# A new order for the seven products of a Winograd tile in the first feed-forward layer, with the scheduler free to order the pair's instructions

## The chip, the core and the metric

The kernel runs on one core of one Trainium2 chip. A core has four engines that compute, and each works through its own list of instructions in order: TensorE (PE in the rows; PEld are its weight loads), VectorE (DVE), ScalarE (ACT) and GpSimd (POOL). SyncE (SP) only starts transfers; GpSimd starts some too. Matrix products go into PSUM, which the kernel uses as eight tiles of one bank each (128 partitions x 512 fp32). Time is the device time of one launch in microseconds (us). The kernel before took 2807.16 us, the median of 3 runs (2806.87 to 2811.38).

## The reference, cut to what matters

One layer of a diffusion backbone works on 256 latent tokens and 256 context tokens of width 2048. The change lies in the first feed-forward half-step, which both groups of tokens go through with the same weights:

```
gate, up = jnp.split(h @ w_in, 2, axis=-1)        # w_in: 2048 x 11264
return (jax.nn.silu(gate) * up) @ w_out
h  = h  + 0.5 * mod[:, 2] * swiglu(modulate(h,  norm_ffn1, mod[:, 0], mod[:, 1]), w_ffn1_in, w_ffn1_out)
hc = hc + 0.5 * mc[2]     * swiglu(modulate(hc, norm_ffn1, mc[0],  mc[1]),  w_ffn1_in, w_ffn1_out)
```

After it come a mixer (linear attention beside a convolution), a second feed-forward half-step for the latent tokens, and a norm.

## The kernel before, in words

**Products in three passes.** Every fp32 operand is split into a high part that TensorE takes at its fast rate and a low remainder. One product of a 128x128 weight block is three matmuls (`mm3`): high by high, high by low, low by high. For weights, ScalarE casts 128x1024 values into a tile `whi` and VectorE subtracts to get `wlo`; `split_next` does this. There are three such buffers (NW = 3), so the cast for a product can begin when the product three places earlier is through on TensorE.

**The pairs.** Hidden tiles 11 to 43 (33 of the 44 tiles of 128 hidden columns) are computed by `pair_tile`. The two token groups and the two halves of the width make a 2x2 block matrix; gate and up weights by the two halves of the width make another. Winograd's scheme multiplies them with seven products of blocks in place of eight. Each product is 8 weight blocks by 3 matmuls, 24 matmuls of 256 columns. Here the products are called product 0 to product 6 by their place in the order. `plan` (line 864) names for each its bank (`a`, `b` or `c`) and its token factor; `Pair.PARTS` (line 103) names its weight factor. Some token factors are sums, kept in the tiles `s` (only product 4, factor `s3`, reads tiles of that name in this stage).

**Intermediate results.** Bank `a` accumulates across four products and is read in between: `late(i)`, run after product i, copies it to SBUF (`S.copy`) or combines it on VectorE. The next matmuls into `a` must wait until that reading is done.

**Weight factors.** A pair has two raw tiles of 128x2048, unit 0 (gate) and unit 1 (up). `t1` is a ScalarE copy of a gate block to which GpSimd's queue adds an up block by an accumulating transfer; `t2` is `t1` plus the up block "22" by VectorE, and later plus the gate block "21"; `t3` is an accumulating transfer into unit 1. `make_t1` and `make_t3` start these for the next pair while the present one runs. There are four raw slots (NRAW = 4). When a unit is used up, `leave` frees its slot and `load` lets SP fetch the next unit. Between the products of a pair lies a "j" step: one 128x2048 row block of the modulation weights takes a raw slot too, and one VectorE instruction multiplies and sums it (`wide_step`, the tile `wcol`).

**What sets the order.** The program is written step by step: the matmuls of product i, then the cast and subtraction for product i+3, then `late(i)`. A scheduler may move instructions against this order. In the kernel before, `pin[0]` (lines 316 and 321) is set during a pair's steps, and then every instruction that goes through `Clocked` (line 64, which is why nearly all rows carry L64) is kept in program order.

Of the kernel before, what the change touches and what calls it, by code (L numbers as in the profile page):

```python
# [18 lines left out]
KT = 16  # L19
T = 256  # L20
# [79 lines left out]
class Pair:  # L100


    PARTS = ("11", "21", "t1", "t2", "t3", "22", "t4")

    def __init__(self, wg, wu):
        self.units = (Unit(wg, 2048), Unit(wu, 2048))
# [3 lines left out]
        self.up_low = wu[:, 0:1024]  # L110
        self.parts = self.PARTS
        self.t = {}
# [3 lines left out]
def layer_kernel(ctx: ExitStack, tc: tile.TileContext, A):  # L116
    nc = tc.nc
    keep = tc.keep_in_program_order
    pin = [False]
    V, PE, S = (  # L120
        Clocked(e, p, keep, pin)
        for e, p in ((nc.vector, _price_dve), (nc.tensor, _price_pe), (nc.scalar, lambda *a: 0.0))
    )
# [13 lines left out]
    def gt(p="g", dt=F32, shape=(128, 512), n=512):  # L137
        t = gpool.tile([128, 2 * (T + 2)], dt, tag="g", name=nm(p))[:, :n]
        return t if len(shape) == 2 else t.rearrange("p (a t) -> p a t", a=shape[1])

    def pst():
        return pspool.tile([128, 512], F32, tag="ps", name=nm("ps"))
# [19 lines left out]
    def m_load():  # L162
        m = mload
        while m["n"] < min(m["used"] + m["ahead"], len(m["srcs"])):
            raw = mraw()
            nc.sync.dma_start(out=raw, in_=m["srcs"][m["n"]])
            m["raw"][m["n"]] = raw
            m["n"] += 1
# [4 lines left out]
    def run():  # L173
        halves = [(u, i) for k, u, i, _ in steps if k == "w"]
        order, pos = [], 0

        def leave(u):
            nonlocal used
            ring["free"].append(ring["at"].pop(u))
            used += 1  # L180
            return raws.pop(u)
# [23 lines left out]
        def load(upto):  # L205
            nonlocal nload
            while nload < min(upto + ring["n"], len(order)):
                u = order[nload]
                raw = raw_tile(u)
                nc.sync.dma_start(out=raw[:, : u.n], in_=u.src)  # L210
                raws[u] = raw
                nload += 1
# [4 lines left out]
        def block(u, b):  # L217
            raw = raws[u.units[int(b[1]) - 1]]
            o = 1024 * (int(b[0]) - 1)
            return raw[:, o : o + 1024]  # L220
# [26 lines left out]
        def pair_after(u, b):  # L247
            nonlocal used
            if b == "t2":
                V.tensor_tensor(out=u.t["t2"], in0=u.t["t2"], in1=block(u, "21"), op=ALU.add)  # L250
            if b in ("t2", "22"):
                leave(u.units[b == "22"])
                load(used)
                later = order[order.index(u.units[1]) + 1 :][:3]
                for x in later:
                    if x.pair is not None and x.pair is not u:
                        (make_t1 if b == "t2" else make_t3)(x.pair)
                        break

        def split_next(early=False):  # L260
            nonlocal pos, used
            if pos >= len(halves):
                return
            u, i = halves[pos]
            pos += 1
            if isinstance(u, Pair):
                m, src = 1024, factor(u, u.parts[i])
            else:
                h0, m = u.parts[i]
                src = raws[u][:, h0 : h0 + m]  # L270
            b = (pos - 1) % NW
            hi = wpool.tile([128, 1024], F32R, tag=f"whi{b}", bufs=1, name=nm("whi"))
            lo = wpool.tile([128, 1024], F32R, tag=f"wlo{b}", bufs=1, name=nm("wlo"))
            c = S.copy(out=hi[:, :m], in_=src)
            d = V.tensor_tensor(out=lo[:, :m], in0=src, in1=hi[:, :m].bitcast(F32), op=ALU.subtract)
            if early:
                keep(c)
                keep(d)
            ready[u, i] = (hi, lo)
            if isinstance(u, Pair):  # L280
                pair_after(u, u.parts[i])
            elif i == len(u.parts) - 1:
                leave(u)
                for x in order[order.index(u) + 1 :][:3]:
                    if x.pair is not None and x in raws:
                        (make_t1 if x is x.pair.units[0] else make_t3)(x.pair)
                load(used)
# [8 lines left out]
        for k, u, i, fn in steps:  # L296
            late = None
            if k == "p":
                fn()
            elif k == "s":  # L300
                split_next(True)
                begun += 1
            elif k == "j":
                fn(raws[u])
                leave(u)
                load(used)
            elif k == "m":
                fn(mload["raw"].pop(i))
                mload["used"] += 1
                m_load()  # L310
            else:
                while begun < NW:
                    split_next(True)
                    begun += 1
                hi, lo = ready.pop((u, i))
                pin[0] = isinstance(u, Pair)
                late = fn(hi, lo)
                split_next()
                if late:
                    late()  # L320
                pin[0] = False
            if k == "w" and slow:
                rate["credit"] += rate["r"]
                while slow and rate["credit"] >= 1:
                    rate["credit"] -= 1
                    slow.popleft()()
            V.t = max(V.t, PE.t - LAG)
            while bg and V.t + bg[0][0] <= PE.t:
                bg.popleft()[1]()
# [40 lines left out]
    def split(src, n=512):  # L370
        hi, lo = gt("hi", F32R), gt("lo", F32R)
        lows(hi[:, :n], lo[:, :n], src)
        return hi, lo
# [244 lines left out]
    wide = deque((c, k) for c in (6, 7, 5, 8) for k in range(KT))  # L618
# [203 lines left out]
    ps2, s3, qf = {}, {}, {}  # L822
# [38 lines left out]

    def pair_tile(f, wg, wu):
        box = {}
        plan = (("a", "11"), ("c", "12"), ("b", "p"), ("a", "s2"), ("a", "s3"), ("b", "q"), ("a", "22"))

        def late(i):
            a, b, c = (box.get(x) for x in "abc")
            if i == 0:
                box["s"], box["u"] = gt("ps"), gt("pu")
                S.copy(out=box["s"][:, :T], in_=a)  # L870
            elif i == 1:
                t = box["s"][:, :T]
                V.tensor_tensor(out=t, in0=c, in1=t, op=ALU.add)
                S.activation(t, t, AF.Silu)
            elif i == 2:
                S.copy(out=box["u"][:, :T], in_=b)
            elif i == 3:
                S.copy(out=box["s"][:, T:], in_=a)
            elif i == 4:
                t = box["u"][:, :T]  # L880
                V.tensor_tensor(out=t, in0=t, in1=a, op=ALU.subtract)
            elif i == 5:
                t = box["s"]
                p = box["p"] = gt("p")
                V.tensor_tensor(out=t[:, T:], in0=b, in1=t[:, T:], op=ALU.subtract)
                V.tensor_tensor(out=p[:, :T], in0=t[:, :T], in1=t[:, T:], op=ALU.mult)
            else:
                t, p = box["u"], box["p"]
                S.activation(t[:, T:], a, AF.Silu)
                V.tensor_tensor(out=p[:, T:], in0=t[:, :T], in1=t[:, T:], op=ALU.mult)  # L890
                hid[f] = split(p)
                keep_hid(f)
                if f // CH_FT < NCH - 1:
                    del hid[f]

        def part(i):
            key, x = plan[i]

            def fn(hi, lo):
                first = key not in box  # L900
                if first:
                    box[key] = pst()[:, :T]
                for j in range(HK):
                    mm3(box[key], (hi, lo), j * 128, x_factor(x, j), first and j == 0, j == HK - 1, not first)
                return lambda: late(i)

            return fn

        u = Pair(wg, wu)
        for i in range(7):  # L910
            steps.append(("w", u, i, part(i)))
            if i == 3 and len(wide) > 2 * KT:
                wide_step()


# [30 lines left out]
    def keep_hid(f):  # L946
        hi, lo = hid[f]
        hid_d[f] = [dpool.tile([128, 512], F32, tag=f"hid{f}_{i}", name=nm("hidd")) for i in range(2)]
        for d, t in zip(hid_d[f], (hi, lo)):
            nc.gpsimd.dma_start(out=d, in_=t.bitcast(F32))  # L950
# [170 lines left out]
    plan = [(0, c) for c in seq0] + [(1, c) for c in seq1]  # L1121
# [730 lines left out]
    for f in range(2, FT):  # L1852
        a = f < NF2
# [10 lines left out]
    for dt in range(KT):  # L1864
        box = {}
# [38 lines left out]

    P(finish)
    run()


# [121 lines left out]
```

## Time and profile before

| | |
|---|---|
| median of 3 runs | 2807.16 us |
| the profiled execution | 2808.95 us |
| its span, first to last instruction | 2807.1 us |
| TensorE busy in the span | 2699.7 us (96%) |
| VectorE, ScalarE, GpSimd busy | 1878.1, 1119.7, 187.2 us |
| mean granted TensorE clock | 0.98 of full speed |

The profiled execution is one run, 1.8 us above the median; its span leaves 1.85 us outside. The granted clock is 1.00 at 2.4 GHz and 0.50 at 1.2 GHz; a value between them is a stretch that holds both. Ends of matmuls are modelled, so the distance between their starts is the better measure.

### The profile page before, as it was taken

The page shows a single profiled execution, that of the slowest core. Times are in us where ns is not written, and L with a number is a line of the kernel's source. Part 1 is how long each engine was busy: PE and PEld are TensorE (multiplying, and loading weights), DVE is VectorE, ACT ScalarE, POOL GpSimd, SP SyncE. Part 2 cuts the span into 40 slices and gives each one's busy share as a digit, 9 for nine tenths or more (in the row PEclk, how much of TensorE's full clock was granted, in tenths as well). Part 3 has the DMA queues.
Part 4 walks back from the last instruction along what each step waited for, and adds up shares of the span by engine and source line. Part 5 has one row for each costly group of instructions (what it writes and reads, how often), then busy time and mean ns, then how long its engine had stood idle before and what let it go on. Part 6 is the DMA issues. An engine that isn't in the chain of part 4 may idle for free.

```text
span 2807.1 us, 45740 instructions
## 1 busy us (share of the span) xinstructions
PE 2699.7 (96%) x18964; PEld 2488.9 (89%) x18964; DVE 1878.1 (67%) x2553; ACT 1119.7 (40%) x1498; POOL 187.2 (7%) x212
## 2 busy tenths in 40 slices
PE   7999999999999999999999899999999999999998
PEld 5668899999999998888888898879999999999998
DVE  6657866666666665479789897767776655444444
ACT  5234444444444443112112554435554444444443
POOL 0002211111111110001001110000100000000000
PEclk9999999999999999999999999999999999999999
DMA  9844577777677678966986442635557765555553
GB/s 366 300 156 168 141 210 200 210 209 217 202 205 208 203 207 319 393 225 243 396 293 222 164 175 69 216 134 213 183 180 275 282 252 188 188 181 182 189 183 122
DMA packets 126635, 608.33 MB, mean 217 GB/s; under 512 B 14682, under 2 KB 15066, under 8 KB 78172
## 3 DMA queue, kind: packets, MB, share of 16 engines
q1 hardware_dynamic: 109308, 546.69, 55.2%
q0 software_dynamic: 16544, 57.68, 9.4%
q8 instruction: 148, 2.42, 0.3%
q10 hardware_dynamic: 576, 1.05, 0.1%
q14 instruction: 59, 0.48, 0.0%
HBM read 580.20 MB, written 25.17 MB: 216 GB/s over the span
## 4 chain that ended last, share of the span: by engine, by line
PE 32%; issue 27%; DVE 2%; DMA 1%; ACT 0%; POOL 0%; POOLq 0%; DVEq 0%; ACTq 0%
PE ps L64 32%; DVE wlo L64 1%; DMA raw<-in_wg 0%; DVE y L64 0%; DVE junk L64 0%; ACT whi L64 0%; DMA raw<-in_wmodT 0%; DVE E L64 0%; DVE S L64 0%; DVE raw L64 0%; DVE xs L64 0%; POOL h L1901 0%; DVE lo L64 0%; DVE h L64 0%; ACT y L64 0%
## 5 line engine op out<-in xcount | busy, mean ns | idle before, releaser
L64 PE MATMUL ps<-hi,whi 128*128 128x256 f32 (+1 forms) x4736 | 1445.4, 307 | 7.8 <-DVE h L64 3.3
L64 PE MATMUL ps<-lo,whi 128*128 128x256 f32 (+1 forms) x4736 | 1448.5, 306 | 2.7 <-DVE lo L64 2.7
L64 PE MATMUL ps<-hi,wlo 128*128 128x256 f32 (+1 forms) x4736 | 1445.9, 306 | 3.8 <-DVE wlo L64 3.7
L64 DVE TENSOR_TENSOR wlo<-raw,whi 128x1024 fp32r<-128x1024 f32 (+1 forms) x654 | 803.9, 1230 | 662.3 <-ACT whi L64 657.0
L64 ACT CAST whi<-raw 128x1024 fp32r<-128x1024 f32 (+1 forms) x654 | 679.2, 1039 | 1276.7 <-PE ps L64 1239.0
L64 PEld LDWEIGHTS ps<-hi,whi 128*128 128x128 f32 x4736 | 895.1, 189 | 65.7 <-issue 11.9
L64 PEld LDWEIGHTS ps<-lo,whi 128*128 128x128 f32 x4736 | 895.3, 189 | 50.4 <-DVE lo L64 2.9
L64 PEld LDWEIGHTS ps<-hi,wlo 128*128 128x128 f32 x4736 | 893.8, 189 | 49.8 <-DVE wlo L64 4.7
L64 DVE CUSTOM_DVE_ANT_0 junk<-mraw,mraw 128x1024 bf16<-128x1024 f32 x192 | 239.0, 1245 | 6.5 <-DMA mraw<-in_wmodT 2.9
L64 PE MATMUL ps<-hh,wlo 128*128 128x256 f32 x704 | 198.2, 282 | 0.0
L64 PE MATMUL ps<-hh,whi 128*128 128x256 f32 x704 | 197.8, 281 | 0.0
L64 PE MATMUL ps<-hl,whi 128*128 128x256 f32 x704 | 197.5, 281 | 0.0
L64 PE MATMUL ps<-s,whi 128*128 128x256 f32 x528 | 131.3, 348 | 59.2 <-ACT ps L64 59.2
L64 PEld LDWEIGHTS ps<-s,whi 128*128 128x128 f32 x528 | 108.6, 253 | 65.7 <-ACT ps L64 65.7
L64 DVE TENSOR_TENSOR wlo<-t,whi 128x1024 fp32r<-128x1024 f32 x99 | 121.3, 1225 | 66.4 <-ACT whi L64 66.4
L64 ACT CAST whi<-t 128x1024 fp32r<-128x1024 f32 x99 | 103.7, 1047 | 122.4 <-DVE t L64 63.0
L64 PEld LDWEIGHTS ps<-hh,whi 128*128 128x128 f32 x704 | 132.9, 189 | 0.0
L64 PEld LDWEIGHTS ps<-hl,whi 128*128 128x128 f32 x704 | 132.6, 188 | 0.0
L64 PEld LDWEIGHTS ps<-hh,wlo 128*128 128x128 f32 x704 | 132.5, 188 | 0.0
L64 DVE TENSOR_TENSOR part<-ps,part 128x512 f32<-128x512 f32 x112 | 72.6, 685 | 66.2 <-PE ps L64 66.0
L64 PE MATMUL ps<-s,wlo 128*128 128x256 f32 x264 | 91.3, 346 | 0.0
L64 DVE TENSOR_TENSOR t<-t,raw 128x1024 f32<-128x1024 f32 x66 | 80.6, 1221 | 1.1
(206 smaller groups left out, 1984.2 us busy)
## 6 DMA issues: line engine op xcount, KB each, us to landing
raw<-in_w2b SPq DMA_DIRECT2D x84, 1024.0 KB, 4.9
raw<-in_w1b SPq DMA_DIRECT2D x72, 1024.0 KB, 7.1
raw<-in_wmodT SPq DMA_DIRECT2D x64, 1024.0 KB, 6.5
mraw<-in_wmodT SPq DMA_DIRECT2D x96, 512.0 KB, 5.6
raw<-in_w1o SPq DMA_DIRECT2D x47, 1024.0 KB, 6.9
mraw<-in_wmodK SPq DMA_DIRECT2D x64, 512.0 KB, 7.6
raw<-in_w2o SPq DMA_DIRECT2D x32, 1024.0 KB, 4.9
hi<-hidd SPq DMA_DIRECT2D x80, 256.0 KB, 6.3
```

Source lines behind the costliest of these rows:

```text
L64: i = f(*a, **k)
```

## The change

The seven products of a pair are put in another order, in which no two neighbours use one bank; the weight factors, the freeing of the raw slots, the "late" work and the place of the modulation step follow that order. The setting of `pin` for pairs is taken out, so that the scheduler orders the pairs' instructions on TensorE, VectorE and ScalarE as it does elsewhere.

```diff
-    PARTS = ("11", "21", "t1", "t2", "t3", "22", "t4")
+    PARTS = ("11", "t1", "t2", "21", "t3", "22", "t4")
...
             if b == "t2":
+                make_next(u, make_t1)
+            elif b == "21":
                 V.tensor_tensor(out=u.t["t2"], in0=u.t["t2"], in1=block(u, "21"), op=ALU.add)
-            if b in ("t2", "22"):
+            if b in ("21", "22"):
                 leave(u.units[b == "22"])
                 load(used)
-                later = order[order.index(u.units[1]) + 1 :][:3]
-                for x in later:
-                    if x.pair is not None and x.pair is not u:
-                        (make_t1 if b == "t2" else make_t3)(x.pair)
-                        break
+                if b == "22":
+                    make_next(u, make_t3)
+
+        def make_next(u, make):
+            for x in order[order.index(u.units[1]) + 1 :][:3]:
+                if x.pair is not None:
+                    make(x.pair)
+                    break
...
-                pin[0] = isinstance(u, Pair)
...
-        plan = (("a", "11"), ("c", "12"), ("b", "p"), ("a", "s2"), ("a", "s3"), ("b", "q"), ("a", "22"))
+        plan = (("a", "11"), ("b", "p"), ("a", "s2"), ("c", "12"), ("a", "s3"), ("b", "q"), ("a", "22"))
...
             elif i == 1:
+                S.copy(out=box["u"][:, :T], in_=b)
+            elif i == 2:
+                S.copy(out=box["s"][:, T:], in_=a)
+            elif i == 3:
                 t = box["s"][:, :T]
                 V.tensor_tensor(out=t, in0=c, in1=t, op=ALU.add)
                 S.activation(t, t, AF.Silu)
-            elif i == 2:
-                S.copy(out=box["u"][:, :T], in_=b)
-            elif i == 3:
-                S.copy(out=box["s"][:, T:], in_=a)
...
-            if i == 3 and len(wide) > 2 * KT:
+            if i == 1 and len(wide) > 2 * KT:
                 wide_step()
```

On TensorE, the kernel before, at the end of product 3 (factor s2) and the start of product 4 (factor s3) of a pair in the middle of the stage. The bank is `ps_3350` in both:

```order
L64 MATMUL ps_3350<-hi_2557,whi_3377 128x256
L64 MATMUL ps_3350<-lo_2558,whi_3377 128x256
L64 MATMUL ps_3350<-hi_2557,wlo_3378 128x256
L64 MATMUL ps_3350<-s_2175,whi_3415 128x256
L64 MATMUL ps_3350<-s_2176,whi_3415 128x256
```

On TensorE, the changed kernel, the end of product 1 and the start of product 2 of the same pair. Its banks are `a` = `ps_3355`, `b` = `ps_3390` and `c` = `ps_3455`:

```order
L64 MATMUL ps_3390<-lo_2558,whi_3305 128x256
L64 MATMUL ps_3390<-hi_2557,wlo_3306 128x256
L64 MATMUL ps_3455<-hi_1323,whi_3380 128x256
L64 MATMUL ps_3455<-lo_1324,whi_3380 128x256
L64 MATMUL ps_3355<-hi_2171,whi_3338 128x256
L64 MATMUL ps_3355<-lo_2172,whi_3338 128x256
```

The scheduler has put the first two matmuls of product 3 (bank `c`) ahead of product 2; the other 22 follow product 2. In the same way the first two matmuls of product 5 stand ahead of product 4 and the other 22 behind it. So TensorE's order in a pair is now: product 0 (24 matmuls), 1 (24), two of 3, 2 (24), 22 of 3, two of 5, 4 (24), 22 of 5, 6 (24).

On ScalarE, the kernel before, from the cast for product 4 to that for product 6 of the same pair and on to the copy of product 3's result (`ps_3387` is the SBUF tile `box["s"]`):

```order
L64 CAST whi_3415<-raw_3148 128x1024
L64 ACTIVATE ps_3387<-ps_3387 128x256
L64 CAST whi_3446<-raw_3148 128x1024
L64 COPY pu_3388<-ps_3421 128x256
L64 CAST whi_3478<-t_3375 128x1024
L64 COPY ps_3387<-ps_3350 128x256
```

On ScalarE, the changed kernel, from the cast for product 2 of that pair to the cast for product 6:

```order
L64 CAST whi_3338<-t_3336 128x1024
L64 ACTIVATE pu_3154<-ps_3121 128x256
L64 COPY t_3342<-raw_3217 128x1024
L64 CAST whi_3380<-raw_2983 128x1024
L64 CAST hi_3347<-p_3309 128x512
L64 COPY ps_3387<-ps_3355 128x256
L64 CAST whi_3415<-raw_3151 128x1024
L64 COPY pu_3388<-ps_3390 128x256
L64 CAST whi_3447<-raw_3151 128x1024
L64 COPY ps_3387<-ps_3355 128x256
L64 CAST whi_3480<-t_3336 128x1024
```

The second copy into `ps_3387` is the one that product 4 waits for. It stood behind the cast for product 6 (`whi_3478`) and now stands ahead of it (`whi_3480`), behind the cast for product 5 (`whi_3447`). The copy that begins the next pair's `t1` (`t_3342`) now stands ahead of the cast for product 3 (`whi_3380`).

## Rows read from the trace of the kernel before

**Rows 1.** The page, its first line.

```profile
span 2807.1 us, 45740 instructions
```

**Rows 2.** Waits: engine, line waited for, us in total, times, longest.

```profile
PE ps L64 <- ACT ps L64: 59.2, 33, 1.8
```

**Rows 3.** TensorE's timeline, one pair: start us, us, operation, idle before, releaser.

```profile
810.25 0.28 PE L64 MATMUL ps<-lo,whi 128*128 128x256 f32 x1
810.37 0.28 PE L64 MATMUL ps<-hi,wlo 128*128 128x256 f32 x1
812.45 0.51 PE L64 MATMUL ps<-s,whi 128*128 128x256 f32 x2 [1.80 <-ACT ps L64]
...
816.92 0.28 PE L64 MATMUL ps<-hi,whi 128*128 128x256 f32 x1
...
833.93 0.28 PE L64 MATMUL ps<-hi,wlo 128*128 128x256 f32 x1
```

**Rows 4.** TensorE's busy time, granted clock, DMA share, GB/s by microsecond.

```profile
811.00:812.00 1.00, 0.00 (x0) 1.00 1.05 262
...
814.00:815.00 1.00, 1.00 (x6) 0.50 0.99 344
...
817.00:818.00 1.00, 1.00 (x11) 1.00 1.05 279
```

**Rows 5.** TensorE's timeline: first and last of the 33 waits, and one between.

```profile
329.19 0.51 PE L64 MATMUL ps<-s,whi 128*128 128x256 f32 x2 [1.62 <-ACT ps L64]
...
374.63 0.51 PE L64 MATMUL ps<-s,whi 128*128 128x256 f32 x2 [1.80 <-ACT ps L64]
...
377.55 0.28 PE L64 MATMUL ps<-hi,whi 128*128 128x256 f32 x1
...
1068.10 0.51 PE L64 MATMUL ps<-s,whi 128*128 128x256 f32 x2 [1.79 <-ACT ps L64]
```

**Rows 6.** ScalarE's timeline around the wait of rows 3.

```profile
805.43 1.04 ACT L64 COPY t<-raw 128x1024 f32<-128x1024 f32 x1
...
809.88 1.03 ACT L64 CAST whi<-raw 128x1024 fp32r<-128x1024 f32 x1
810.81 0.36 ACT L64 COPY pu<-ps 128x256 f32<-128x256 f32 x1
811.08 1.04 ACT L64 CAST whi<-t 128x1024 fp32r<-128x1024 f32 x1
812.02 0.37 ACT L64 COPY ps<-ps 128x256 f32<-128x256 f32 x1
817.06 1.05 ACT L64 CAST whi<-raw 128x1024 fp32r<-128x1024 f32 x1 [4.67 <-PE ps L64]
```

**Rows 7.** VectorE's timeline in the same pair.

```profile
806.82 1.23 DVE L64 TENSOR_TENSOR t<-t,raw 128x1024 f32<-128x1024 f32 x1
...
813.29 2.29 DVE L64 CUSTOM_DVE_ANT_0 raw<-raw,sc 128x2048 f32<-128x2048 f32 x1
...
818.14 1.23 DVE L64 TENSOR_TENSOR wlo<-raw,whi 128x1024 fp32r<-128x1024 f32 x1 [2.55 <-ACT whi L64]
```

**Rows 8.** DMA issues, 330 to 1070 us and then 815.0 to 815.8: KB each, median us to landing.

```profile
raw<-in_w1b SPq DMA_DIRECT2D x62, 1024.0 KB, 7.2
...
raw<-in_w1b POOLq DMA_DIRECT2D x32, 512.0 KB, 8.9
...
raw<-in_w1b SPq DMA_DIRECT2D x1, 1024.0 KB, 8.6
```

**Rows 9.** Two stretches: busy of PE, PEld, DVE, ACT, POOL, clock, DMA share, GB/s.

```profile
330.00:1070.00 740.00, 682.46 (x5385) 675.28 (x5384) 496.66 (x548) 322.50 (x447) 93.19 (x127) 0.95 0.71 205
1900.00:2340.00 440.00, 438.33 (x3680) 434.42 (x3679) 305.19 (x396) 208.39 (x275) 13.83 (x13) 1.00 0.64 228
```

**Rows 10.** The first pair: timelines of TensorE and of ScalarE.

```profile
321.13 0.28 PE L64 MATMUL ps<-lo,whi 128*128 128x256 f32 x1
321.85 0.39 PE L64 MATMUL ps<-hi,wlo 128*128 128x256 f32 x1 [0.44 <-DVE wlo L64]
...
321.22 1.04 ACT L64 CAST whi<-t 128x1024 fp32r<-128x1024 f32 x1
322.17 1.05 ACT L64 COPY t<-raw 128x1024 f32<-128x1024 f32 x1
```

## The prediction

> **What bounds the kernel now.** I began with the page's first line and the list of waits. The span is 2807.1 us [rows 1]; the profiled execution took 2808.95 us, 1.85 outside its span and 1.8 above the median of the runs, so I make the sum against 2808.95 and take 1.8 off at the end. TensorE is busy nearly throughout, so only what makes it wait or slows it counts. One wait has the shape of the change: TensorE waits 33 times, once in each pair, at a matmul into a PSUM bank for ScalarE, 59.2 us in all [rows 2]. The timeline of one pair shows the place: the last matmul of product 3 starts at 810.37, the first of product 4 at 812.45 [rows 3]. ScalarE's rows show why it is long: when product 3 ends, ScalarE still finishes a cast, then copies `pu`, then casts for product 6 (1.04 us), and only then copies bank `a` (812.02, 0.37 us) [rows 6].
>
> The wait is not the whole loss. Read by the microsecond, the granted clock is 1.00 while TensorE is idle, is at 0.50 by 814, after TensorE has started again, and is back at 1.00 by 817 [rows 4]. So product 4 runs mostly at 1.2 GHz: from 812.45 to 816.92 it takes 4.47 us [rows 3]; in a pair where the clock did not fall, it takes 374.63 to 377.55, or 2.92 us [rows 5]. No such fall stands in the stretch from 1900 to 2340, where TensorE is busy 438.33 of 440 us and the clock is 1.00; in the pairs it is 0.95 on the mean [rows 9].
>
> **What a pair costs, and what it would cost without the wait.** From the first of the 33 waits to the last are 32 periods: (1068.10 - 329.19) / 32 = 23.09 us [rows 5]. The undisturbed pace: from 816.92 to 833.93 are 143 steps of one matmul, 17.01 us, or 0.119 us a step [rows 3]. A product of 24 matmuls is 2.85 us, and a pair of 168 matmuls 19.98 us. The loss is 3.11 us a pair: 2.08 - 0.12 = 1.96 us of gap, and 1.15 us of slow clock on the mean (1.62 where it falls, almost nothing where it doesn't, which makes seven pairs in ten).
>
> **The change, part by part.**
>
> *The order of products.* It removes the neighbours on bank `a`. Between product 2 (s2) and product 4 (s3) there are now 24 matmuls into other banks, 2.85 us; count time from the first matmul of a pair. Product 2 ends at 8.80. ScalarE starts a cast 0.14 us after a product ends (816.92 against 817.06 [rows 3, 6]): cast for product 5 from 8.94 to 9.99, then the copy, done by 10.4. Product 4 starts at 11.66. The wait is gone, with 1.3 us to spare. If that cover were gone, each us of delay would be a us of gap.
>
> *Other places where a bank is read.* `b` is copied after product 1 and not touched before 11.42; `c` has no later product in the pair; bank `a` is read by VectorE after product 4 (14.51) and written again at 17.13, which leaves 2.6 us for one short instruction. These cost nothing.
>
> *The hoisted matmuls.* Two matmuls of product 3 now stand ahead of product 2, at 5.71. They need the cast for product 3, which may begin when product 0 is through (2.85). ScalarE's list ahead of it is: the cast for product 2 (0.14 to 1.19), an activation out of PSUM (some 0.37, as the copies), the copy into `t1` (1.04) [rows 6]. That ends near 2.6. So the cast runs from 2.99 to 4.04: 1.67 us to spare, and VectorE's subtraction (1.23 [rows 7]) ends near 5.3, wanted at 8.80. No cost in the steady state. The same two matmuls as head of the line are the point to doubt. The Trainium skill (PSUM — Partial Sum Buffer, Engine vs sequencer instructions) says that matmuls start and complete in program order and that ScalarE's queue is strictly first in, first out. By that rule a late `t1` copy would hold back the cast, the cast two matmuls, and these the whole of product 2, though product 2 needs none of them; the rows here show the ScalarE half of it (a copy waiting behind a cast [rows 6]). If everything is in time, rule and sum give the same; the second rival below prices the case in which it is not.
>
> *The earlier weight factors.* The `t1` copy needs the raw tile that SP loads into the slot of unit 1, freed by the subtraction for product 5. VectorE reaches it after the subtraction for product 4 (cast 5.85 to 6.9, done 8.1) and the modulation step, which now lies here (2.29 [rows 7], to 10.4): done at 11.65. The load then belongs to the pair after next, and the copy comes in the next pair, at 19.98 + 1.56 = 21.54. It lands 7.2 us after its issue as a rule, 8.6 beside the other transfers [rows 8]: 18.9 to 20.3. SP's list ahead of it holds unit 1 of the next pair (freed about 5.3) and a modulation block (10.4), both issued by then. Unit 1 lands at 12.5; VectorE wants it for `t2` near 18, and GpSimd's accumulation for `t3` (8.9 us [rows 8]) ends near 21.5, wanted by the cast for product 4 at 25.8. Nothing reaches TensorE.
>
> *The engines' load.* In the stage VectorE is busy 496.66 of 740 us, ScalarE 322.50, the DMA engines 0.71 [rows 9]. Per pair that is 15.5, 10.1 and 16.4 us, so with a period of 19.98 they stand at 78%, 50% and 82%. None becomes the bound.
>
> *The first pair.* Here the factors don't have a pair's time ahead. In the rows of before product 2 begins about 321.0 and waits 0.44 us at its third matmul; the cast for `t2` runs at 321.22 and the copy into the next `t1` at 322.17 [rows 10]. Now both stand ahead of the cast for product 3: 322.17 + 1.05 + 1.05 = 324.3, while TensorE wants it about 321.0. That is a new wait of about 3.3 us, with 0 to 1.6 us of slow clock behind it; gone are the 0.44 and the first pair's own 1.62 [rows 5]. Net 1.2 to 2.8 us lost; I take 2.
>
> *No longer pinned.* Beyond the hoisting it changes the order of a few matmuls after the pairs, where TensorE has other work ready. I take 0, within 3 us either way.
>
> **The sum.** 32 x 3.11 = 99.5 us gained, less 2: 97.5. 2808.95 - 97.5 = 2711.4, and against the median 1.8 less: 2710 us, 3.5% faster. Own range: with the pace of pure matmul steps (0.118) and no loss in the first pair it is 2704; if each of the four new seams per pair costs 0.1 us (13 us), it is 2723; with 3 us beyond the pairs, 2701 to 2726.
>
> **The rivals.**
> 1. *The gap goes, the clock does not come back.* The low clock would have another cause than the gap, say the load of the stage. For it: in about three pairs of ten the same gap costs no clock. Against: in [rows 4] the low clock follows the gap within 3 us and has ended 3 us later, and a stage as dense runs at 1.00 [rows 9]. Gain 32 x 1.96 = 62.7 less 2: 2746 us.
> 2. *The hoisted matmuls become the new wait; slower at its far end.* Place: two matmuls of product 3, behind the cast, the `t1` copy, and the load that it waits for. TensorE waits once the load takes more than 21.54 - 11.65 + 1.67 = 11.6 us; it took 8.6. The DMA engines go from 0.71 to 0.82 and three loads now start closer together, which speaks for it; 2.9 us of slack speaks against. Price: each us of gap 32 us, and about 37 more for the clock. A gap of 1 us gives 2710 + 32 + 37 = 2779. From a gap of 3.11 - 1.15 = 1.96 us, that is a landing of 13.5 us, the kernel is no faster than before; 3 us would give 2843. By the Trainium skill (DMA: Bandwidth & Descriptors, Issuing engines are not separate DMA queues) transfers of SP and GpSimd run on the same 16 engines and interleave; that is why I count with the landing beside others.
> 3. *The wait only moves.* Product 4 waits for the same copy, if ScalarE comes to it over 1.3 us late, for example held at the cast for product 4 by a late `t3`. That needs the accumulation to land more than 4 us late [rows 8], and a full loss of 3.11 us a pair a good deal more: 2807 us.
>
> **Chances.** Forecast 0.78; rival 1 0.07; rival 2 with a short gap (2730 to 2800) 0.08, with a gap past the turning point 0.03; rival 3 0.02 and, between them, something outside the pairs that eats part of the gain 0.02. Within 0.2% (5.6 us, about what a measurement of this kernel can tell from no change) there is little room between these cases. So faster 0.94, same 0.02, slower 0.04. The range is 2700 to 2746: the forecast's own and rival 1's value; what lies above it holds under 2 in 10.
>
> **What would show it.** Right: the row of TensorE's waits for ScalarE at a bank, 33 times, is gone or holds one or two; the start-to-start distance of pairs is 19.9 to 20.1 us; the clock is 1.00 through the stage except in the first pair; the stage is about 98 us shorter and no other stage moves by more than 3. Product 4 takes 2.85 us in every pair. In the first pair a wait of some 3 us at the first matmul of product 3, released by ScalarE's cast. Wrong: a wait in each pair at that matmul with ScalarE's `t1` copy waiting for a load (rival 2), at product 4 (rival 3), or pairs without gaps at a clock below 1.00 (rival 1). The most likely error of size is the seams: a tenth of a us at each place where a product is split.

## The result, and the profile after

The changed kernel takes 2703.73 us, the median of 3 runs (2703.02 to 2709.08), against 2807.16 before: a ratio of 0.9633, 95% interval 0.9609 to 0.9656, or 103 us less. The forecast was 2710 us with a range of 2700 to 2746. The profiled execution took 2703.02 us.

The first line of the page, and the list of TensorE's waits from 310 to 980 us (engine, what it waited for, us in total, times, longest), stand against [rows 1, 2]:

```profile
span 2701.3 us, 45665 instructions
...
PE ps L64 <- ACT whi L64: 2.8, 2, 2.6
PE ps L64 <- DVE wlo L64: 1.0, 1, 1.0
PE ps L64 <- ACT ps L64: 0.2, 1, 0.2
```

The row of 33 waits and 59.2 us is down to one wait of 0.2 us. The two rows above it are of the first pair alone. TensorE's timeline of the pair at the place of [rows 3] shows product 4 without a gap ahead of it: its first matmul starts at 806.17, 0.11 us behind the one before, and the next product's at 809.00, 2.83 us later, where it was 4.47 [rows 3]:

```profile
806.06 0.28 PE L64 MATMUL ps<-lo,whi 128*128 128x256 f32 x1
806.17 0.40 PE L64 MATMUL ps<-s,whi 128*128 128x256 f32 x2
...
809.00 0.28 PE L64 MATMUL ps<-hi,wlo 128*128 128x256 f32 x1
```

The first and the last product 4 of the 33 pairs, in the same view, and then the stretch between them (columns as in [rows 9]):

```profile
328.38 0.40 PE L64 MATMUL ps<-s,whi 128*128 128x256 f32 x2
...
965.27 0.40 PE L64 MATMUL ps<-s,whi 128*128 128x256 f32 x2
```

```profile
330.00:965.00 635.00, 634.80 (x5362) 634.58 (x5361) 493.40 (x544) 325.02 (x445) 93.17 (x127) 1.00 0.81 238
```

A pair now takes (965.27 - 328.38) / 32 = 19.90 us instead of 23.09 [rows 5]. TensorE is busy in 634.80 of 635 us at a clock of 1.00, where it had 0.95 [rows 9]. The profiled executions differ by 2808.95 - 2703.02 = 105.9 us: 738.91 - 636.89 = 102.0 between the first and the last product 4, 0.8 ahead of them, 3.0 behind them, and 0.1 outside the spans. The gain lies in the pairs. The 0.8 us are two things: the first pair starts 1.4 us earlier (312.15 against 313.58), for the most part because a wait of TensorE some 29 us into the kernel was shorter (0.6 us against 1.9), and the pair itself loses 0.6. Of the 3.0, some 1.6 are the last pair's slow clock, and 2.1 a wait of TensorE for VectorE's tile `lo` behind the pairs, 2.7 us before and 0.6 now; the clock in other gaps there gives a little back. e4 and e7 below change nothing behind the pairs and have 2.7 us at that wait again, so these 2.1 us are not shown to come from the change.

One execution of e7 below took 5258.91 us, nearly twice the others; its ratio leaves it out, and nothing on record shows the cause.

### The profile page after: what moved, and what is told of

Read it like the earlier page. It is cut to its first block, busy times and chain, and to the rows that moved or that the text cites. A ratio compares the mean times of both kernels' runs of the same rounds, so it can differ in the third digit from the quotient of the medians.

```text
span 2701.3 us, 45665 instructions
## 1 busy us (share of the span) xinstructions
PE 2654.8 (98%) x18964; PEld 2450.7 (91%) x18964; DVE 1878.8 (70%) x2553; ACT 1123.8 (42%) x1498; POOL 188.2 (7%) x212
## 4 chain that ended last, share of the span: by engine, by line
PE 57%; issue 28%; DVE 2%; DMA 0%; ACT 0%; POOL 0%; POOLq 0%; ACTq 0%; DVEq 0%
PE ps L64 57%; DVE wlo L64 1%; DMA raw<-in_w1b 0%; DVE y L64 0%; DVE junk L64 0%; ACT whi L64 0%; DVE E L64 0%; DVE h L64 0%; DVE lo L64 0%; POOL h L1905 0%; DVE raw L64 0%; DVE xs L64 0%; POOLq L2029 0%; ACT L64 0%; DVE t L64 0%
## 5 line engine op out<-in xcount | busy, mean ns | idle before, releaser
L64 PE MATMUL ps<-s,whi 128*128 128x256 f32 x528 | 94.6, 280 | 0.0
L64 PEld LDWEIGHTS ps<-s,whi 128*128 128x128 f32 x528 | 80.5, 188 | 0.0
L1032 POOL TENSOR_TENSOR nacc<-nacc,sq 128x512 f32<-128x512 f32 x19 | 37.3, 1979 | 572.5 <-ACT sq L64 572.3
```

The source lines that it names most:

```text
L64: i = f(*a, **k)
L1032: eng.tensor_tensor(out=acc, in0=acc, in1=sq, op=ALU.add)
```

## The experiments

There were twelve runs in three groups (e1 to e4, e5 to e8, e9 to e12), each group beside the kernel before on the same chip. The ratios are to that kernel; the period is the mean distance between the first and the last product 4, read from one profiled execution as above, and the last column is the mean granted clock of the pairs from 330 us on.

| run | what it is | ratio (95% interval) | period, us | clock |
|---|---|---|---|---|
| the change | | 0.9633 (0.9609 to 0.9656) | 19.90 | 1.00 |
| e1 | new order, still pinned | 0.9715 (0.9700 to 0.9729) | 20.61 | 1.00 |
| e2 | old order, not pinned | 0.9961 (0.9946 to 0.9976) | 22.76 | 1.00 |
| e3 | old order, pinned, the late copy ahead of a cast | 0.9785 (0.9771 to 0.9800) | 21.30 | 1.00 |
| e4 | the change, cast for product 3 done twice | 0.9650 (0.9634 to 0.9666) | 20.07 | 1.00 |
| e5 | the change, `t1` copy behind the cast for product 3 | 0.9760 (0.9747 to 0.9774) | 20.99 | 1.00 |
| e6 | the change, modulation step put back | 0.9670 (0.9657 to 0.9683) | 20.07 | 1.00 |
| e7 | the change, modulation block loaded twice | 0.9639 (0.9624 to 0.9653) | 19.89 | 1.00 |
| e8 | e1, two reads of bank `a` ahead of casts | 0.9660 (0.9646 to 0.9673) | 20.08 | 1.00 |
| e9 | e6, two loads exchanged | 0.9636 (0.9622 to 0.9650) | 19.90 | 1.00 |
| e10 | e8, two loads exchanged | 0.9628 (0.9614 to 0.9642) | 19.84 | 1.00 |
| e11 | the change again | 0.9635 (0.9619 to 0.9651) | 19.90 | 1.00 |
| e12 | e10, `t1` copy behind the cast for product 3 | 0.9621 (0.9607 to 0.9636) | 19.83 | 1.00 |

### The two halves of the change, each alone (e1, e2)

e1 puts the pin back:

```diff
                 hi, lo = ready.pop((u, i))
+                pin[0] = isinstance(u, Pair)
                 late = fn(hi, lo)
```

> The changed kernel with the pair's instructions kept in program order again, so the new order of products without the hoisting of two matmuls. My theory (the order of products takes the gap and with it the slow clock away): the 33 waits of TensorE for ScalarE at product 4 stay gone, pairs 19.9 to 20.0 us apart, 2700 to 2710 us. Rival (the scheduler's freedom is what gains, the order alone does not): waits come back and the time lies above 2740 us.

It came out between the two expectations, at 2729.58 us, 23 us above the changed kernel (0.0082 of 2807): the order in program order gives 2.5 of the 3.2 us a pair. TensorE's timeline of a pair shows the rest as two short gaps, at the first matmul of product 6 (706.15) and of product 2 (715.04); with them the rows of VectorE and ScalarE that end just before:

```profile
705.80 0.28 PE L64 MATMUL ps<-hi,wlo 128*128 128x256 f32 x1
706.15 0.36 PE L64 MATMUL ps<-hi,whi 128*128 128x256 f32 x1
...
714.62 0.28 PE L64 MATMUL ps<-hi,wlo 128*128 128x256 f32 x1
715.04 0.38 PE L64 MATMUL ps<-hi,whi 128*128 128x256 f32 x1
...
704.45 1.22 DVE L64 TENSOR_TENSOR wlo<-raw,whi 128x1024 fp32r<-128x1024 f32 x1 [1.42 <-ACT whi L64]
705.60 0.41 DVE L64 TENSOR_TENSOR pu<-pu,ps 128x256 f32<-128x256 f32 x1
...
713.68 1.04 ACT L64 CAST whi<-raw 128x1024 fp32r<-128x1024 f32 x1
714.63 0.36 ACT L64 COPY ps<-ps 128x256 f32<-128x256 f32 x1
```

Both are reads of bank `a` that stand in the program behind a longer subtraction or cast: 705.60 + 0.41 = 706.01, then product 6; 714.63 + 0.36 = 714.99, then product 2. The scheduler of the changed kernel had put each read ahead. The new order removes the neighbours on bank `a`, but between the two products that share it there is only one other product, 2.85 us, and a cast or subtraction that begins late, with the read behind it, overruns that.

e2 takes only the pin out of the kernel before:

```diff
-                pin[0] = isinstance(u, Pair)
```

> The kernel before with nothing changed but the pinning taken out. The scheduler then puts product 5 (bank b) between products 3 and 4 by itself, and 21 matmuls of the next pair between 4 and 6. My theory says that any 24 matmuls into other banks between products 3 and 4 cover the copy (it needs about 1.6 us after product 3), whoever puts them there: 2700 to 2720 us. Rival (the new order of products is needed): 2780 us or more, with the wait for ScalarE still in each pair.

The expectation failed. The wait at bank `a` is gone, since the scheduler moves product 5 between products 3 and 4, but little is gained by it. TensorE's waits from 330 to 1062 us, which are nearly all of the stage, and the stretch:

```profile
PE ps L64 <- ACT whi L64: 35.4, 54, 1.0
PE ps L64 <- DVE wlo L64: 28.2, 31, 1.0
PE ps L64 <- DVE pu L64: 3.5, 4, 1.0
PE ps L64 <- ACT pu L64: 0.7, 1, 0.7
...
330.00:1058.00 728.00, 660.58 (x5376) 642.10 (x5376) 484.65 (x547) 324.85 (x447) 93.30 (x127) 1.00 0.70 208
```

67.8 us of waits where there were 59.2 [rows 2], 63.6 of them for casts and subtractions: matmuls moved ahead come to TensorE before their weights are cast. The clock stays at 1.00, and 0.3 us a pair is what the freedom alone is worth. The two halves are not a sum of independent terms: 0.3 and 2.5 alone, 3.2 together.

### Is the slow clock the gap's price? (e3)

e3 shortens the gap and leaves the order as it was:

```diff
                 late = fn(hi, lo)
+                if isinstance(u, Pair) and i == 3:
+                    late()
+                    late = None
                 split_next()
```

> The kernel before, pinned, with one edit: after product 3 ScalarE copies bank a before the cast for product 6, not after it. The neighbours on bank a stay. The copy should end about 0.95 us earlier, so the gap shrinks from 1.80 to some 0.85 us of idle time in each pair. Theory a (the slow clock is a price of the gap that a shorter gap pays less often or not at all): 2807 - 31 for the gap, and up to 37 more for the clock: 2739 to 2776 us. Theory b (the clock falls for another reason than the gap): 2776 us and product 4 still 4.4 to 4.5 us in about seven pairs of ten.

TensorE's waits, and the stretch with its clock:

```profile
PE ps L64 <- ACT ps L64: 27.4, 32, 0.9
...
330.00:1020.00 690.00, 660.38 (x5430) 647.56 (x5430) 498.36 (x553) 325.00 (x449) 93.28 (x127) 1.00 0.78 224
```

The gap falls by 0.94 us (1.80 to 0.86), the period by 1.79 (23.09 to 21.30): the 0.85 above the gap's own 0.94 is slow clock that is no longer paid, though a gap remains in every pair. The kernel before shows the same price directly: 9 of its 32 periods are 22.0 us and 23 are 23.4 to 23.6, so a fall of the clock costs 1.5 us, 1.1 on the mean. (e3 gives back some 0.3 of it at a new seam, the start of product 6.) This speaks against rival 1 by itself: the stage is denser than before and the clock is full.

### How much room do the moved matmuls have? (e4, e5, e7)

e4 casts the weights of product 3 twice, which holds ScalarE some 1 us longer:

```diff
             c = S.copy(out=hi[:, :m], in_=src)
+            if isinstance(u, Pair) and u.parts[i] == "21":
+                for _ in range(1):
+                    c = S.copy(out=hi[:, :m], in_=src)
             d = V.tensor_tensor(out=lo[:, :m], in0=src, in1=hi[:, :m].bitcast(F32), op=ALU.subtract)
```

> The changed kernel with ScalarE's cast for product 3 made twice in each pair (1.05 us more). This eats the slack that I reckoned for the two hoisted matmuls (1.67 us). My sum: the second cast ends near 5.6 us after the pair's start, wanted at 5.7, and the copy of product 0 behind it near 5.95, wanted at 5.95: no change to at most 0.3 us a pair, 2703 to 2715 us. Rival (the chain has no slack left, the kernel stands right at the edge): 1 us of gap in each pair and the slow clock behind it, 2740 to 2775 us.

The cost is 0.17 us a pair on the mean, but not in each: most periods are still 19.89, six of them 20.2 to 21.4. The time, 2711.55 us, is in the range expected; the mean hides that a few pairs pay it all. In five of the six the copy that starts the next `t1` waits for its load to land. ScalarE's row of one such pair, and TensorE's row that follows from it:

```profile
381.27 1.05 ACT L64 COPY t<-raw 128x1024 f32<-128x1024 f32 x1 [2.12 <-DMA raw<-in_w1b]
...
384.79 0.39 PE L64 MATMUL ps<-hi,whi 128*128 128x256 f32 x1 [1.25 <-ACT whi L64]
```

The changed kernel itself has such waits, at 11 of 32 copies, of up to 1.98 us. The longest one, in ScalarE's and TensorE's timelines of the changed kernel, with the load's issue on SP and its landing (DMA issues from 328.45 to 328.75: KB, us to landing):

```profile
340.08 1.05 ACT L64 COPY t<-raw 128x1024 f32<-128x1024 f32 x1 [1.98 <-DMA raw<-in_w1b]
342.51 0.36 ACT L64 COPY ps<-ps 128x256 f32<-128x256 f32 x1
...
342.33 0.28 PE L64 MATMUL ps<-hi,whi 128*128 128x256 f32 x1
342.45 0.28 PE L64 MATMUL ps<-lo,whi 128*128 128x256 f32 x1
342.92 0.39 PE L64 MATMUL ps<-hi,whi 128*128 128x256 f32 x1 [0.20 <-ACT ps L64]
```

```profile
328.55 0.33 SPq L210 DMA_DIRECT2D raw<-in_w1b  x1
...
raw<-in_w1b SPq DMA_DIRECT2D x1, 1024.0 KB, 11.5
```

It was issued at 328.55 and landed 11.5 us later, and 0.20 us of that reached TensorE. The prediction put the limit at 11.6 us. But the place is another one: the two moved matmuls (342.33 and 342.45) had their cast in time, and what waited is the first matmul of product 2, for ScalarE's copy of bank `a` behind product 0 (342.51), which stands behind the late `t1` copy and two casts. In e4, where the cast for product 3 is made twice, it is the moved matmuls that wait. So the changed kernel runs with nearly no room there, and a microsecond of extra work on ScalarE (e4) is paid mostly in the pairs whose load is late.

e7 tried to reach the limit with traffic: each modulation block of the pairs is loaded a second time.

```diff
                 nc.sync.dma_start(out=raw[:, : u.n], in_=u.src)
+                if u.pair is None and order[nload - 1].pair is not None and u.n == 2048 and nload + 1 < len(order) and order[nload + 1].pair is not None:
+                    nc.sync.dma_start(out=raw[:, : u.n], in_=u.src)
```

> The changed kernel with each modulation block of the pairs loaded twice into the same buffer: 1 MB more of traffic for a pair, on top of 4.74 MB (151.17 MB in 31.9 periods), and no other work. The transfers now take 0.81 of a period; by the same rate (16.1 us for 4.74 MB) they would take 19.5 us of 19.89. Theory a: the landing of the next pair's first block is the next limit (ScalarE's copy of it waits for the landing by 0.2 to 2.0 us in a dozen pairs already, and the one that waited 1.98 cost TensorE 0.20): landings get longer by some us, TensorE waits for the cast behind that copy in most pairs, period 20.2 to 21.5 us, 2713 to 2755 us. Theory b: the loads are issued far enough ahead and the copies' waits stay under 1.8 us: period 19.9 us, 2700 to 2708 us.

Its stretch, and three loads in SP's list:

```profile
330.00:965.00 635.00, 635.00 (x5366) 634.99 (x5365) 493.71 (x545) 325.36 (x446) 93.18 (x127) 1.00 0.94 289
...
747.25 0.33 SPq L210 DMA_DIRECT2D raw<-in_wmodT  x1
748.39 0.33 SPq L210 DMA_DIRECT2D raw<-in_w1b  x1
753.29 0.33 SPq L212 DMA_DIRECT2D raw<-in_wmodT  x1
```

With the DMA engines at 0.94 and 289 GB/s in place of 0.81 and 238, TensorE loses nothing; 8 of 32 copies wait, 1.58 us at most. Expectation (b) held: so much more traffic on the mean does not make the load late. It does not clear traffic in general. The second copy of the modulation block goes out some 5 us behind the load in question (753.29 against 748.39), so the added megabyte stands behind that load on the queue, not ahead of it.

e5 moves the copy out of the way of the cast:

```diff
-            if b == "t2":
+            if b == "21":
                 make_next(u, make_t1)
-            elif b == "21":
                 V.tensor_tensor(out=u.t["t2"], in0=u.t["t2"], in1=block(u, "21"), op=ALU.add)
```

> The changed kernel with ScalarE's copy of the next pair's first block put behind the cast for product 3 instead of ahead of it. Theory a: in the first pair TensorE waits 2.58 us for that cast, of which the copy is 1.04, so the wait is 1.5 to 1.7 us there; in the other pairs a late landing no longer holds up the cast for product 3. Gain 1 us at the start and at most 0.2 us elsewhere: 2701 to 2704 us, the same within what a median tells. Theory b: the copy now delays the cast for the product after, or comes too late for the next pair's first cast: period over 20.0 us and 2707 us or more.

The first pair's wait is shorter as expected (2.58 to 1.64 us), but each later pair but the last loses 1.1 us: 2741.93 us, within the bound of (b), but by a path that neither expectation named. The scheduler, which goes by its own estimates, now puts 22 matmuls of product 3 ahead of product 2, then product 2, the last two of product 3, two of product 5, and product 4. The cast for product 5 may begin only when product 2 is through, and the two matmuls of product 5 stand almost directly behind it. ScalarE's and TensorE's rows:

```profile
749.61 1.04 ACT L64 CAST whi<-raw 128x1024 fp32r<-128x1024 f32 x1 [4.19 <-PE ps L64]
...
750.71 0.39 PE L64 MATMUL ps<-hi,whi 128*128 128x256 f32 x1 [0.84 <-ACT whi L64]
```

This is the mechanism of rival 2, matmuls put ahead that hold up what stands behind them, released by another cast than the one it named. Its gap, 0.84 us in nearly all of them, is seen in 31 pairs, and the clock stays at 1.00 there.

### Why the load is late (e6, e9, e8, e10)

e6 puts one part of the change back, the place of the modulation step:

```diff
-            if i == 1 and len(wide) > 2 * KT:
+            if i == 3 and len(wide) > 2 * KT:
```

> The changed kernel with the modulation block's step put back behind the fourth product, as it was before. Theory a: TensorE is busy without a gap in the pairs and neither the DMA queues nor VectorE set its pace, so the place of that step is worth nothing: 2700 to 2708 us, period 19.9 us. Theory b: the step's 2.3 us on VectorE, or its load's new place on the queue, delays a subtraction or the load of the next pair in the second half of the pair: 0.3 us a pair or more, 2712 us or more.

It costs 10 us (0.0037 of 2807). The profiled executions differ by 11.0 us: 2714.07 - 2703.02. Of that 5.3 lie between the first and the last product 4; 2.6 lie ahead of them, where the clock fell in the first pair, as it did in e11, which has no edit at all; and 3.1 behind them, where the wait for `lo` is 2.7 us again, as in e4 and e7. So 5.3 us, or 0.17 a pair, are shown to be the edit's; the total fits (b), the 0.3 us a pair does not. Beside e7, whose first pair and wait for `lo` are like e6's, 5.8 of the 6.6 us between the two profiles lie in the pairs. In the pairs 14 of 32 copies wait for the load, by up to 2.77 us, and TensorE pays where that is most. SP's rows, ScalarE's and TensorE's in one such pair:

```profile
774.51 13.72 SPq L210 DMA_DIRECT2D raw<-in_w1b  x2
...
784.62 1.05 ACT L64 COPY t<-raw 128x1024 f32<-128x1024 f32 x1 [2.77 <-DMA raw<-in_w1b]
...
786.67 0.38 PE L64 MATMUL ps<-hi,whi 128*128 128x256 f32 x1 [0.66 <-ACT whi L64]
```

The load goes out at 774.51 (the first of the two in the row), when VectorE is through with the modulation step. In pairs where the copy doesn't wait it stands 7.3 us behind the issue; in the changed kernel it is 9.8.

e9 keeps the step where e6 has it and exchanges the two loads in SP's list, so that the raw block goes out ahead of the modulation block, 10.2 us ahead of its copy:

```diff
+        for n in range(len(order) - 2, 0, -1):
+            if order[n].pair is None and order[n - 1].pair is not None and order[n + 1].pair is not None:
+                order[n], order[n + 1] = order[n + 1], order[n]
         raws, ready = {}, {}
```

> The modulation block's step behind the fourth product again, but the first raw block of the pair after next is fetched ahead of the modulation block and no longer behind it, so that it goes out when VectorE's subtraction for product 5 is through and not after the modulation step: about 3 us earlier against the copy that needs it (7.3 us ahead of it with the step put back alone, 9.8 in the changed kernel). Theory a: the 10 us that putting the step back cost are late landings of this load; then they are gone, no more than a few copies wait for it, and the ratio is 0.9625 to 0.9645. Theory b: they come from the step's 2.3 us on VectorE: then the waits stay and the ratio is 0.966 or more.

No copy waits any more, each period from the second pair on is 19.9 us, and the ratio is the changed kernel's, although the wait for `lo` behind the pairs stays at 2.4 us. So what e6 loses in the pairs is the load, not the 2.3 us on VectorE. More than the issue has moved: DMA issues of one such load in e9 (751.3 to 751.6), to be read against the changed kernel's 11.5:

```profile
751.43 0.33 SPq L213 DMA_DIRECT2D raw<-in_w1b  x1
...
raw<-in_w1b SPq DMA_DIRECT2D x1, 1024.0 KB, 5.2
```

Over the 23 of these loads whose landing a profile gives, it is 9.8 us in the median in the changed kernel (7.5 to 11.5) and 6.1 in e9 (5.0 to 7.4). Before the change it was 7.9 (6.4 to 9.6). e9 differs from the changed kernel in the place of the step too; where the exchange is all that differs, the median goes from 7.5 (e6) to 6.1 (e9), and from 9.1 (e8 below) to 7.0 (e10). In the changed kernel the load is issued 1.13 us behind a modulation block of the same size on the same queue, and lands 4.3 us after that block in the median. The Trainium skill (DMA: Bandwidth & Descriptors, Queues, rings and completion order) says that each DMA engine takes the descriptors of a queue in order; these landings agree. The block ahead is not all of it: in e5 the load goes out 3.3 us behind the block, as it did before the change (3.4), and yet takes 9.6 us where it took 7.9. There a GpSimd load of 512 KB has gone out 1.4 us ahead of it, and an earlier GpSimd transfer is still under way. GpSimd's loads move with every one of these edits, and no run holds them fixed.

e8 is e1 with the two late reads moved ahead of the cast and subtraction that held them:

```diff
                 late = fn(hi, lo)
+                if late and i in (0, 4):
+                    late()
+                    late = None
                 split_next()
```

> The new order with every matmul left at its program place (as in the run that kept the pin), and the reads of bank a behind products 0 and 4 written ahead of the next cast and subtraction. Theory a: the 0.67 us that a pair loses with the pin are two seams, 0.31 where VectorE's subtraction that reads bank a stands behind another subtraction, and 0.41 where ScalarE's copy of product 0 stands behind a cast; freeing the scheduler repairs them and nothing else. Then this run has a period of 19.9 to 20.1 us and 2703 to 2711 us in all, with no wait of PE at the two places. Theory b: the free order hides other waits too (casts that come late at the places where it starts two matmuls of the next product early), which come back here: period over 20.3 us and 2718 us or more.

Where no load is late a pair takes 19.83 us, which is 168 steps of 0.118: both seams of e1 are closed. But ten waits of 0.2 to 1.0 us follow late landings, since in program order there is less room behind the copy (a wait of 1.40 us at the copy costs 1.02 here, one of 1.98 cost 0.20 in the changed kernel). So each expectation held in part: the scheduler's order had closed the seams and, besides, hidden most of the late landings. e10 adds the exchange of the loads:

> The new order in program order, with the two reads of bank a ahead of the casts, and the same exchange of the two loads: the block goes out 1.1 us earlier (10.4 us ahead of its copy instead of 9.3). Theory a: the 7 us over the changed kernel that this arrangement showed are its 10 waits for a late landing, each over 0.4 us of slack; an earlier issue takes away those under 1.1 us and shortens the rest: ratio 0.9625 to 0.9645, period 19.83 us. Theory b: the landing goes with the issue of the block on the other queues, and is late by the same amount: ratio 0.966 again.

All 32 periods are 19.83 to 19.90, no copy waits, and the load lands in 7.0 us in the median, as (a) said. This is the changed kernel's time without a free scheduler: the unpinning is one way to these 0.7 us, not the only one.

### The change again, and a last variant (e11, e12)

> The changed kernel itself, run again as the measure for the other kernels of this group: ratio 0.9625 to 0.964, period 19.9 us, and a few of ScalarE's copies of the next pair's first block wait for its landing (11 of 32 in the first profile, 1.98 us at most).

The same ratio, and 7 of 32 copies that wait, up to 1.84 us. e12 puts the `t1` copy behind the cast for product 3, as e5 did, but in program order:

> The kernel before it in this group (program order, reads first, block fetched first), and ScalarE's copy of the block put behind the cast for product 3. In program order no matmul of product 3 is moved ahead of product 2, which was what cost 1.1 us a pair when the copy was moved in the changed kernel. Theory a: a late landing then holds up only the cast for product 4, with more slack, and the first pair gains 1 us: 2 to 4 us under the changed kernel, ratio 0.9615 to 0.9635. Theory b: the copy delays the read of product 1 or the cast for product 4: a new wait of TensorE in every pair, period over 20 us, ratio over 0.965.

Every period is 19.83 and the median 2701.85 us against 2705.75 of the change beside it; the intervals (0.9607 to 0.9636, 0.9619 to 0.9651) overlap, so it isn't shown to be faster. The 1 us of the first pair was not seen: its waits are 1.88 and 0.49 us, as in e10. What it has is room: no copy waits for a load.

## Why the prediction held, step by step

- **The wait and its removal**: right. The copy of s2 is in time in every pair.
- **The slow clock as the gap's price**: right, shown by e3 (0.86 us of gap, no slow clock) and by the change; 1.15 us on the mean was forecast, 1.1 is read from the periods of before. Rival 1 is out.
- **The pace, 19.98 us**: mis-sized by 0.08. The 0.119 us a step came from the 143 steps of one pair [rows 3]; undisturbed pairs take 19.89 with split products and 19.83 without. That is 32 x 0.08 = 2.6 us. The seams it feared (0.1 us each) are 0.06 a pair in all.
- **The last pair's slow clock**: left out. The sum counts 32 periods, but there were 33 gaps; the last is worth some 1.6 us more. With the pace (2.6), the first pair (2 forecast, 0.6 lost: 1.4), its start (1.4 us earlier, not forecast and not shown to be the change's) and 1.4 us more behind the pairs this makes the 8.4 us between the forecast for the profiled execution, 2711.4, and its 2703.02.
- **The first pair, 2 us lost**: the wait came where it was put, 2.58 us at the two moved matmuls for a forecast of 3.3. From the start of product 0 to that of product 4 the first pair takes 15.61 us before (313.58 to 329.19) and 16.23 in this execution (312.15 to 328.38), in which the clock did not fall: 0.6 lost. In the second (e11) it fell, and the pair takes 17.83 (312.92 to 330.75): 2.2 lost. The forecast of 1.2 to 2.8 holds for that one.
- **The room behind the `t1` load**: mis-sized, and it is partly luck that it cost nothing. The prediction took a landing of 7.2 us from the median of all loads on the line, and 8.6 from one of them [rows 8]. By its own times this load goes out 1.25 us behind a modulation block (10.4 and 11.65), where it was 3.4 before, and it gave that no price; it took 9.8, up to 11.5. The limit of 11.6 us came out near, but not by its own working: the chain through the cast for product 3 had 0.4 us more than it counted (the copy ends near 2.6, the cast starts at 2.99), and ScalarE's copy of bank `a` behind product 0, which gave out first, is neither in it nor among the bank reads that the prediction lists. Rival 2 was nearer than the 2.9 us of slack said, and e4, e6 and e8 show less room costing 5 to 10 us.
- **Rival 2's price**: too high for a short gap. It put 37 us of slow clock on a gap of 1 us in each pair; e5 has 31 gaps of 0.84 to 1.12 us and no slow clock behind them.
- **The modulation step's place at no cost**: held only because the step went along. With the step left where it was (e6), the change would have lost some 5 us in the pairs, and 10 of its 103 us by the medians.
- **No longer pinned, taken as 0 within 3 us**: behind the pairs it was in that range, in them the premise was wrong, though not the total. The 3.11 us a pair were laid to the order alone, and e1 shows that the order in program order gives 2.5; two reads of bank `a` there stand behind a cast and a subtraction. The prediction worked out all its times from the scheduled order, where these reads were already ahead, so it priced both edits as one and gave the whole of it to the first.
- **The engines' load**: DMA share 0.81 where 0.82 was forecast; in e7 0.94 was not too much.

What stays open: why the same load lands in 7.5 us in one pair and in 11.5 in another of the same execution. For these two the trace moves the question one step ahead: the modulation block before them on the queue lands 4.1 us after the load's issue in the first (issue 806.00) and 7.2 in the other (328.55), which is 3.2 of the 4.0 us. Why the block is late is not shown.

## What to carry to other kernels

A wait at a shared PSUM bank is priced as the gap and what the clock loses after it, and it is gone when the read of the bank ends before the one product between is through, so count what stands ahead of the read in its engine's list. One cast that starts when the product ends still fits (the copy of s2 here); a cast or subtraction that starts late does not (e1). When a change moves a load in its queue, take the landing of that load and not the median of its line: what stands just ahead of it on the queue can add some microseconds (2.1 in e8 against e10). Two edits that reach the same instructions (an order and the freedom to reorder) are worth a run each before either is given a price.

## What the runs showed of the hardware

- A gap doesn't always bring the clock down. In the first pair TensorE waits 2.58 us at the same matmul in both executions of the changed kernel, and in e6 and e7 too. In the first the clock stays at 1.00 (TensorE's busy time, granted clock, DMA share, GB/s):

```profile
321.00:323.00 2.00, 0.67 (x5) 1.00 0.36 135
323.00:325.00 2.00, 2.00 (x19) 1.00 0.81 98
325.00:327.00 2.00, 2.00 (x19) 1.00 1.11 236
```

  and in the second (e11) it is at 0.50 by 325, with 11 matmuls in 2 us in place of 19, and back at 1.00 by 328:

```profile
323.00:324.00 1.00, 0.82 (x6) 1.00 0.00 0
325.00:327.00 2.00, 2.00 (x11) 0.50 1.02 176
328.00:329.00 1.00, 1.00 (x11) 1.00 0.91 352
```

  In e6 and e7 it fell as well; in e1 and e4, behind gaps of 2.86 and 2.84 us in the same pair, it did not. In the later pairs gaps of 1.80 us brought it down in about seven of ten [rows 5], gaps of 0.83 to 1.12 us in none of 123 (e2, e3, e5).
- More traffic on the mean did not make transfers land later: from 238 to 289 GB/s the raw loads on SP kept their median (8.6 and 8.5 us). The order of two loads on one queue changed it: 9.1 against 7.0 us (e8, e10) and 7.5 against 6.1 (e6, e9).
